# Scores and value products of two softmax branches grouped by pair of heads, in the attention of the second block

## The chip, the cores and the metric

One Trainium2 chip, one core. The time is the device time of one execution of the whole program in microseconds (us); less is better. Engines are named as in the profile: PE is the matrix engine, PEld its weight loads, DVE the vector engine, ACT the scalar engine, POOL and SP the two others. SBUF is the working memory beside the engines, PSUM the eight banks into which PE writes.

## The reference

Three layers over 256 positions of width 1024: two hybrid layers, then one block of another make. The change lies in that last block. Its mixer has two groups of eight heads of 64. The first group has three branches whose outputs are summed with gates:

```python
p_c = _masked_softmax(einsum('bsgrd,bgnd->bgrsn', qg, kc) * scale, mask_c)       # 15 compressed keys
...
p_s = _masked_softmax(einsum('btgrd,bgtkd->bgrtk', q_b, kg) * scale, mask_s)     # selected blocks
o_s = einsum('bgrtk,bgtkd->btgrd', p_s, vg)
...
p_w = _masked_softmax(einsum('btgrd,bsgd->bgrts', q_b, kwb) * scale, mask_w)     # window
o_w = einsum('bgrts,bsgd->btgrd', p_w, vwb)
...
o = gt[:, :, 0] * o_cmp + gt[:, :, 1] * o_s + gt[:, :, 2] * o_w
```

With 256 positions the four blocks of 64 are all selected and the window of 512 holds everything, so both softmax branches are causal attention over the same 256 positions, each with keys and values of its own. The second group (DSA) scores every position with an indexer, keeps the 64 best for each query, and attends to those. Both groups' outputs go through `w_out`, a norm and a residual, and then a SwiGLU feed-forward part.

## The kernel before

**Products.** Large projections are made as three products of split numbers (hi·hi, lo·hi, hi·lo; lines 276 to 278), 128 x 512 each, with weights that are loaded as `raw`, split into `hi` by ACT (L129) and into `lo` by DVE (L130). They add up in PSUM banks of the pool `acc` (four banks). Scores go to the pool `sc` (two banks, `bank()`), transposes to the pool `pt` (one bank, `bank2()`), and the outputs of a pair of heads to half a bank, `ob`.

**The heads of the first group.** The loop of L1249 takes a pair of heads `j` at a time, and first makes the product of the compressed branch (L1253) into `ob`. That product needs `cp`, which a chain of small steps makes for each half `t` of the positions: scores (L1228), maximum, exponential (L1235), gate (L1241), two transposes of `ce` (L271) into `pt`, copy (L1245). The one buffer `ce` is cleared anew for the second half (L1225). Then for each of the two softmax branches `br`: `pair_scores` makes the scores of two heads, 64 rows of PE's array each (L634 the first 128 queries, L643 the others); `softmax2` adds the mask and takes the maximum on DVE (L339) and the exponential on ACT (L340); a reciprocal and a gate follow (L1261, L1262); `scaled` multiplies, by DVE (L583) and ACT (L581) in turn; `transposed` makes three transposes into `pt` (L271) and a copy to SBUF (ACT, L617, buffer `ptsb`, three of them); `pair_values` makes the value products of the two heads, 64 columns of the array each (L590, L592). One step of the top-64 search of the indexer (DVE, L1209 and L1210) is laid in after each head. `put_pair` (L571 ACT, L572 DVE) takes the result out of `ob`.

**What sets the order.** [...] `pair_scores` and `pair_values` have a raised priority so that their products stay together. Products of other work are laid between them, "fills" below: the query projection of the second group (`dsa_queries`, 48 products into two `acc` banks, called at `j == 2` but placed earlier where it can be) and, later, the output projection (`out_proj`, L1300). After the eight pairs (the loop of L1271 does the same for the second group, with keys `kD`) come the end of `out_proj`, the norms (L928 to L959), and the feed-forward part.

Of the kernel before, what the change touches and what calls it, by code (L numbers as in the profile page):

```python
# [10 lines left out]
F32 = mybir.dt.float32  # L11
# [160 lines left out]
def body(ctx: ExitStack, tc: tile.TileContext, io, out):  # L172
    nc = tc.nc
    V, A, G, T = nc.vector, nc.scalar, nc.gpsimd, nc.tensor
# [16 lines left out]
    def tmp(n=1152):  # L191
        return ln_p.tile([128, 1152], F32, tag="y", name="y")[:, :n]
# [74 lines left out]
    mask = cst[:, C_MASK:C_MASK + 256]  # L267
# [308 lines left out]
    def scaled(e, r, ap):  # L576

        mix[0] += 1
        for t, c in ((0, slice(0, 128)), (1, slice(128, 384))):
            if mix[0] % 2 == 0:  # L580
                A.activation(e[:, c], e[:, c], AF.Copy, scale=r[:, t:t + 1])  # L581
            else:
                V.tensor_scalar(e[:, c], e[:, c], r[:, t:t + 1], None, op0=OP.mult)  # L583
        return transposed(e, ap, False)

    def pair_values(o, pts, v, c0, first, last):

        with tc.high_priority(offset=PRIO):
            for h in (1, 0):
                T.matmul(o[64 * h:64 * h + 64, :], v[:, 0, c0[h]:c0[h] + 64], pts[h][:, 0:256], start=first, stop=False)  # L590
            for h in (1, 0):
                T.matmul(o[64 * h:64 * h + 64, 128:256], v[:, 1, c0[h]:c0[h] + 64], pts[h][:, 256:384], start=False, stop=last)  # L592
# [10 lines left out]
    def pv(o, pt, vb, c0, c1):  # L603
# [2 lines left out]
        T.matmul(o[:, 1, :], pt[:, 128:256], vb[:, 0, c0:c1], start=True, stop=False)  # L606
        T.matmul(o[:, 1, :], pt[:, 256:384], vb[:, 1, c0:c1], start=False, stop=True)

    def transposed(e, ap, eng):
        b = bank2()  # L610
        for i in range(3):
            tr(b[:, i * 128:(i + 1) * 128], e[:, i * 128:(i + 1) * 128])
        pt = ap.tile([128, 384], F32, tag="ptsb", name="ptsb", bufs=3)
        if eng:
            V.tensor_copy(pt, b[:, :384])
        else:
            A.activation(pt, b[:, :384], AF.Copy)  # L617
        return pt
# [7 lines left out]

    last_read = []

    def pair_scores(q, k):

        s = [bank(), bank()]
        with tc.high_priority(offset=PRIO):
            for h in range(2):
                m = T.matmul(s[h][:, 0:128], q(h)[:, 0:128], k(h)[:, 0:128], start=True, stop=True)  # L634
                if h == 0:

                    for i in last_read:
                        tc.add_manual_dep(m.ins, i.ins.name,
                                          mybir.DependencyInfo(mybir.DependencyClass.Sync, mybir.DependencyReason.DATA),
                                          reason="pair")  # L640
                    last_read.clear()
            for h in range(2):
                T.matmul(s[h][:, 128:384], q(h)[:, 128:256], k(h)[:, 0:256], start=True, stop=True)  # L643
        return s

    def softmax2(s, bm, ap, sm):

        e = ap.tile([128, 384], F32, tag="e", name="e", bufs=4)
        nm = small(2)
        softmax_rows(e[:, 0:128], s[:, 0:128], bm[:, 128:256], nm[:, 0:1], sm[0])  # L650
        last_read.append(softmax_rows(e[:, 128:384], s[:, 128:384], bm, nm[:, 1:2], sm[1]))
        return e
# [329 lines left out]
    cos2 = cst[:, C_COS2:C_COS2 + 32].rearrange("p (t c) -> p t c", t=2)  # L982
    sin2 = cst[:, C_SIN2:C_SIN2 + 32].rearrange("p (t c) -> p t c", t=2)
    with tc.tile_pool(name="at2", bufs=1, reuse_waits="tile") as ap:
        hdT = XT()

        def rope2(dst, src, t, n):
# [25 lines left out]
        kSW = ap.tile([128, 2, 256], F32, name="kSW")  # L1013
        vSW = ap.tile([128, 2, 384], F32, name="vSW")
        kc2 = ap.tile([128, 2, 2, 256], F32, tag="kc", name="kc2")
        nq = ap.tile([128, 4, 256], F32, tag="nq", name="nq")
# [37 lines left out]
        def hidden(i, run):  # L1054

            fl = tmp(512).rearrange("p (l c) -> p l c", l=16)
            G.memset(fl[:, :, 30:32], 0.0)
            base = kc2[:, i]
            for g in range(2):
                src = bass.AP(tensor=base.tensor, offset=base.offset + 256 * g,  # L1060
                              ap=[list(base.ap[0]), [2, 16], [16, 15]])
                V.tensor_tensor(fl[:, :, 15 * g:15 * g + 15], src,
                                prm[:, P_PE + 16 * i:P_PE + 16 * i + 16, None].to_broadcast([128, 16, 15]), op=OP.add)

            pp = bank()
            for n in range(16):
                s = n % 4
                T.matmul(pp[32 * s:32 * s + 32, :128], fl[:, n, :], c1[i][:, 128 * n:128 * n + 128], start=n < 4, stop=n >= 12)
            part = ap.tile([128, 128], F32, tag="part", name="part")
            A.activation(part, pp[:, :128], AF.Copy)  # L1070
            ph = bank()
            T.matmul(ph[:, :32], part, cst[:, C_S:C_S + 32], start=True, stop=True)
            run()
            gx = ap.tile([128, 4, 30], F32, tag="gx", name="gx", bufs=2)
            x_, u_, e_, h_ = gx[:, 0], gx[:, 1], gx[:, 2], gx[:, 3]
            V.tensor_scalar(x_, ph[:, :30], prm[:, P_B1 + i:P_B1 + i + 1], None, op0=OP.add)
            V.tensor_tensor(u_, x_, x_, op=OP.mult)
            V.tensor_scalar(u_, u_, 0.044715, 1.0, op0=OP.mult, op1=OP.add)
            V.tensor_tensor(u_, u_, x_, op=OP.mult)
            A.activation(e_, u_, AF.Tanh, scale=math.sqrt(2.0 / math.pi))  # L1080
            V.tensor_scalar(e_, e_, 1.0, 0.5, op0=OP.add, op1=OP.mult)
            V.tensor_tensor(h_, e_, x_, op=OP.mult)
            return h_
# [139 lines left out]
        for t in range(2):  # L1223
# [18 lines left out]
            b = bank2()  # L1242
# [6 lines left out]
        for j in range(4):  # L1249
            if j == 2:  # L1250
                dq = dsa_queries()
            o = obank2()
            T.matmul(o, vcD[:, 2 * (j % 2):2 * (j % 2) + 2, :].rearrange("p s c -> p (s c)"), cp[:, j // 2, :],  # L1253
                     start=True, stop=False)
            for br in range(2):
                ss = pair_scores(lambda h: nq[64 * h:64 * h + 64, j, :], lambda h: kSW[64 * h:64 * h + 64, br, :])
                pts = []
                for h in range(2):
                    sm = small(4)
                    e = softmax2(ss[h], mask, ap, (sm[:, 0:1], sm[:, 1:2]))  # L1260
                    V.reciprocal(sm[:, 2:4], sm[:, 0:2])  # L1261
                    V.tensor_tensor(sm[:, 2:4], sm[:, 2:4], gw[:, :, 8 * (1 + br) + 2 * j + h], op=OP.mult)  # L1262
                    pts.append(scaled(e, sm[:, 2:4], ap))
                    next(top, None)
                pair_values(o, pts, vSW, (128 * (1 + br), 128 * (1 + br) + 64), False, br == 1)
            put_pair(hdT, j, o)

        for _ in top:
# [2 lines left out]
        for j in range(4):  # L1271
            o = obank2()
            ss = pair_scores(lambda h: dq[64 * h:64 * h + 64, j, :], lambda h: kD[64 * h:64 * h + 64, j, :])
            pts = []
# [126 lines left out]
```

## Time and profile before

| | us |
|---|---|
| median of three runs | 968.99 (968.64 to 971.33) |
| the profiled execution | 970.08 |
| its span, first to last instruction | 968.3 |
| PE busy in the span | 935.5 (97%) |
| DVE, ACT busy | 687.4 (71%), 567.8 (59%) |
| mean granted clock of PE | 0.991 of full speed |

The busy times are those of one profiled execution. The scores of the first pair begin at 697.9 us, the last product of `out_proj` is at 768.8 us, and the feed-forward part takes up the rest; what the change moves lies nearly all in these 71 us. Where PE is busy without a gap, the time goes by its work; where it waits, the trace names the instruction it waited for.

### The profile page before, as it was taken

To read this page: it belongs to the slowest core of one execution; us is meant where nothing else is said; L and a number is where in the kernel's file an instruction comes from. 1 tells how busy PE (TensorE), PEld (TensorE's weight loads), DVE (VectorE), ACT (ScalarE), POOL (GpSimd) and SP (SyncE) were. 2 spreads that over 40 slices of the span, in tenths; PEclk is the share of its full clock that TensorE was granted. 3 is DMA by queue.
4 is the path that set the end of the run, shared out by engine and by line. 5 is a ranking of instruction groups with operands and counts; after the bars stand their busy time and mean duration, and the time that the engine had idled before them with its cause. 6 is when DMAs were issued, how large, how long until landed. Compare 5 with 4: busy or idle time off the path is not lost. (4 is left out here: it accounts for less than half of the span.)

```text
span 968.3 us, 14604 instructions
## 1 busy us (share of the span) xinstructions
PE 935.5 (97%) x5418; PEld 785.1 (81%) x5418; DVE 687.4 (71%) x1487; ACT 567.8 (59%) x1143; POOL 28.8 (3%) x54
## 2 busy tenths in 40 slices
PE   8999999999999999999999999889999899999997
PEld 6888688888887888878888888788666698888886
DVE  4648788878788757668877565787788676565654
ACT  4657665555454577656455554555589745454642
POOL 0000010000000100000000000101000100000000
PEclk9999999999999999999999999999999989999999
DMA  9755548887874533447876575365312255546441
GB/s 319 288 100 217 197 175 303 292 296 271 307 253 174 193 131 130 153 176 282 301 284 217 175 255 181 109 238 207 137 45 88 66 174 184 207 169 211 154 163 44
DMA packets 33450, 190.45 MB, mean 197 GB/s; under 512 B 3696, under 2 KB 5346, under 8 KB 15842
## 3 DMA queue, kind: packets, MB, share of 16 engines
q1 hardware_dynamic: 31224, 183.75, 53.5%
q10 hardware_dynamic: 2154, 5.75, 2.1%
q8 instruction: 43, 0.70, 0.3%
q14 instruction: 29, 0.24, 0.1%
HBM read 188.17 MB, written 1.32 MB: 196 GB/s over the span
## 5 line engine op out<-in xcount | busy, mean ns | idle before, releaser
L130 DVE TENSOR_TENSOR lo<-raw,hi 128x1024 fp32r<-128x1024 f32 (+3 forms) x284 | 336.7, 1201 | 92.0 <-ACT hi L129 86.9
L129 ACT ACTIVATE hi<-raw 128x1024 fp32r<-128x1024 f32 (+3 forms) x284 | 290.2, 1038 | 104.7 <-PE acc L278 70.0
L292 PE MATMUL sc<-xh,hi 128*128 128x512 f32 x648 | 198.4, 395 | 0.0
L276 PE MATMUL acc<-hi,xh 128*128 128x512 f32 (+4 forms) x384 | 135.6, 355 | 0.7 <-ACT hi L129 0.7
L277 PE MATMUL acc<-lo,xh 128*128 128x512 f32 (+4 forms) x384 | 134.3, 350 | 0.6 <-DVE lo L130 0.6
L278 PE MATMUL acc<-hi,xh 128*128 128x512 f32 (+4 forms) x384 | 133.7, 350 | 0.7 <-DVE xh L322 0.7
L287 PEld LDWEIGHTS sc<-xh,lo 128*128 128x128 f32 x648 | 110.4, 188 | 21.2
L287 PE MATMUL sc<-xh,lo 128*128 128x256 f32 x648 | 116.0, 281 | 0.0
L292 PEld LDWEIGHTS sc<-xh,hi 128*128 128x128 f32 x648 | 104.9, 189 | 6.8
L276 PE MATMUL acc<-hi,hh 128*128 128x512 f32 x264 | 103.1, 390 | 0.0
L277 PE MATMUL acc<-lo,hh 128*128 128x512 f32 x264 | 103.0, 390 | 0.0
L278 PE MATMUL acc<-hi,hl 128*128 128x512 f32 x264 | 102.6, 390 | 0.0
L292 PE MATMUL pt<-xh,hi 128*128 128x512 f32 x312 | 97.7, 394 | 0.0
L276 PEld LDWEIGHTS acc<-hi,xh 128*128 128x128 f32 x384 | 74.8, 195 | 8.3 <-issue 1.5
L277 PEld LDWEIGHTS acc<-lo,xh 128*128 128x128 f32 x384 | 74.8, 195 | 6.8 <-DVE lo L130 1.4
L278 PEld LDWEIGHTS acc<-hi,xh 128*128 128x128 f32 x384 | 74.3, 194 | 6.5 <-DVE xh L322 1.7
L340 ACT ACTIVATE e<-e,sm 128x128 f32<-128x128 f32 (+1 forms) x128 | 56.8, 446 | 12.0 <-DVE sm L339 7.3
L287 PEld LDWEIGHTS pt<-xh,lo 128*128 128x128 f32 x312 | 53.1, 188 | 10.2
L276 PEld LDWEIGHTS acc<-hi,hh 128*128 128x128 f32 x264 | 49.5, 188 | 11.3 <-ACT hh L481 1.0
L277 PEld LDWEIGHTS acc<-lo,hh 128*128 128x128 f32 x264 | 49.6, 188 | 10.6
L278 PEld LDWEIGHTS acc<-hi,hl 128*128 128x128 f32 x264 | 49.5, 188 | 10.5 <-DVE hl L482 0.3
L414 DVE CUSTOM_DVE_ANT_0 ada<-ada,csil 128x1024 f32<-128x1024 f32 x48 | 56.2, 1220 | 0.0
(287 smaller groups left out, 1302.2 us busy)
## 6 DMA issues: line engine op xcount, KB each, us to landing
raw<-in_w_gate SPq DMA_DIRECT2D x33, 1024.0 KB, 4.9
raw<-in_w_up SPq DMA_DIRECT2D x33, 1024.0 KB, 4.9
raw<-in_w_down SPq DMA_DIRECT2D x33, 1024.0 KB, 4.8
ada<-in_w_ada SPq DMA_DIRECT2D x48, 512.0 KB, 5.7
raw<-in_w_o SPq DMA_DIRECT2D x8, 1024.0 KB, 5.1
raw<-in_w_inaqk SPq DMA_DIRECT2D x6, 1024.0 KB, 5.0
raw<-in_w_inbqk SPq DMA_DIRECT2D x4, 1024.0 KB, 6.9
gb<-in_lnrows ACTq DMA_DIRECT2D x4, 1024.0 KB, 7.1
```

The lines of the kernel that those rows point to most:

```text
L129: self.nc.scalar.activation(hi[:, :n], t[:, c], AF.Copy)
L130: self.nc.vector.tensor_tensor(lo[:, :n], t[:, c], hi[:, :n].bitcast(F32), op=OP.subtract)
L276: T.matmul(dst, lh, rh, start=start, stop=False)
L277: T.matmul(dst, lh, rl, start=False, stop=False)
L278: T.matmul(dst, ll, rh, start=False, stop=stop)
L287: T.matmul(dst[:, 0:256], ws[i][1], xT.hi[:, k0 + i, :], start=False, stop=False)
L292: T.matmul(dst, ws[i][0], xT.pair(k0 + i), start=k0 + i == 0, stop=k0 + i == 7)
L340: A.activation(e, e, AF.Exp, bias=nm, scale=-1.0, accum_out=sm)
L414: V.tensor_tensor_reduce(out=w, in0=w, in1=csil, scale=1.0, scalar=0.0, op0=OP.mult, op1=OP.add, accum_out=modc[:, g:g + 1])
```

## The change

The scores of both branches of a pair go in one run: those of branch 0 to the two `sc` banks, those of branch 1 to two banks of `acc`, held to follow by an added order (`follow`). The four softmaxes come next, and after them the value products of both branches in one run of eight, branch 1 ahead of branch 0. `ptsb` gets a fourth buffer in the second block, and to pay for it `part`, a small tile in the making of the compressed keys, takes a place in the ring `tmp` of three.

```diff
@@ -606,11 +606,13 @@
         T.matmul(o[:, 1, :], pt[:, 128:256], vb[:, 0, c0:c1], start=True, stop=False)
         T.matmul(o[:, 1, :], pt[:, 256:384], vb[:, 1, c0:c1], start=False, stop=True)
 
+    ptsb = [3]
+
     def transposed(e, ap, eng):
         b = bank2()
         for i in range(3):
             tr(b[:, i * 128:(i + 1) * 128], e[:, i * 128:(i + 1) * 128])
-        pt = ap.tile([128, 384], F32, tag="ptsb", name="ptsb", bufs=3)
+        pt = ap.tile([128, 384], F32, tag="ptsb", name="ptsb", bufs=ptsb[0])
         if eng:
             V.tensor_copy(pt, b[:, :384])
         else:
@@ -626,12 +628,18 @@
 
     last_read = []
 
-    def pair_scores(q, k):
+    last_score = [None]
+
+    def pair_scores(q, k, bank=bank, follow=False):
 
         s = [bank(), bank()]
         with tc.high_priority(offset=PRIO):
             for h in range(2):
                 m = T.matmul(s[h][:, 0:128], q(h)[:, 0:128], k(h)[:, 0:128], start=True, stop=True)
+                if h == 0 and follow:
+                    tc.add_manual_dep(m.ins, last_score[0].ins.name,
+                                      mybir.DependencyInfo(mybir.DependencyClass.NoSync, mybir.DependencyReason.DATA),
+                                      reason="pair")
                 if h == 0:
 
                     for i in last_read:
@@ -640,7 +648,7 @@
                                           reason="pair")
                     last_read.clear()
             for h in range(2):
-                T.matmul(s[h][:, 128:384], q(h)[:, 128:256], k(h)[:, 0:256], start=True, stop=True)
+                last_score[0] = T.matmul(s[h][:, 128:384], q(h)[:, 128:256], k(h)[:, 0:256], start=True, stop=True)
         return s
 
     def softmax2(s, bm, ap, sm):
@@ -982,6 +990,7 @@
     cos2 = cst[:, C_COS2:C_COS2 + 32].rearrange("p (t c) -> p t c", t=2)
     sin2 = cst[:, C_SIN2:C_SIN2 + 32].rearrange("p (t c) -> p t c", t=2)
     with tc.tile_pool(name="at2", bufs=1, reuse_waits="tile") as ap:
+        ptsb[0] = 4
         hdT = XT()
 
         def rope2(dst, src, t, n):
@@ -1066,7 +1075,7 @@
             for n in range(16):
                 s = n % 4
                 T.matmul(pp[32 * s:32 * s + 32, :128], fl[:, n, :], c1[i][:, 128 * n:128 * n + 128], start=n < 4, stop=n >= 12)
-            part = ap.tile([128, 128], F32, tag="part", name="part")
+            part = tmp(128)
             A.activation(part, pp[:, :128], AF.Copy)
             ph = bank()
             T.matmul(ph[:, :32], part, cst[:, C_S:C_S + 32], start=True, stop=True)
@@ -1252,17 +1261,20 @@
             o = obank2()
             T.matmul(o, vcD[:, 2 * (j % 2):2 * (j % 2) + 2, :].rearrange("p s c -> p (s c)"), cp[:, j // 2, :],
                      start=True, stop=False)
+            ss = [pair_scores(lambda h: nq[64 * h:64 * h + 64, j, :], lambda h: kSW[64 * h:64 * h + 64, br, :], b, br == 1)
+                  for br, b in ((0, bank), (1, acc))]
+            pts = [[], []]
             for br in range(2):
-                ss = pair_scores(lambda h: nq[64 * h:64 * h + 64, j, :], lambda h: kSW[64 * h:64 * h + 64, br, :])
-                pts = []
                 for h in range(2):
                     sm = small(4)
-                    e = softmax2(ss[h], mask, ap, (sm[:, 0:1], sm[:, 1:2]))
+                    e = softmax2(ss[br][h], mask, ap, (sm[:, 0:1], sm[:, 1:2]))
                     V.reciprocal(sm[:, 2:4], sm[:, 0:2])
                     V.tensor_tensor(sm[:, 2:4], sm[:, 2:4], gw[:, :, 8 * (1 + br) + 2 * j + h], op=OP.mult)
-                    pts.append(scaled(e, sm[:, 2:4], ap))
+                    pts[br].append(scaled(e, sm[:, 2:4], ap))
                     next(top, None)
-                pair_values(o, pts, vSW, (128 * (1 + br), 128 * (1 + br) + 64), False, br == 1)
+
+            for br in (1, 0):
+                pair_values(o, pts[br], vSW, (128 * (1 + br), 128 * (1 + br) + 64), False, br == 0)
             put_pair(hdT, j, o)
 
         for _ in top:
```

PE at the start of the heads. `sc_7034` and `sc_7035` are the scores of the first pair, `acc_7261` is the query projection of the second group, `ce` belongs to the compressed branch. Before:

```order
L1228 MATMUL sc_7012<-kcB_6352,nq_6347 128x32 x4
L276 MATMUL acc_7261<-hi_6891,xh_4674 128x512
L277 MATMUL acc_7261<-lo_6892,xh_4674 128x512
L278 MATMUL acc_7261<-hi_6891,xh_4674 128x512
L634 MATMUL sc_7034<-kSW_6344,nq_6347 128x128
L643 MATMUL sc_7034<-kSW_6344,nq_6347 128x256
L276 MATMUL acc_7261<-hi_6895,xh_4674 128x512
L277 MATMUL acc_7261<-lo_6896,xh_4674 128x512
L278 MATMUL acc_7261<-hi_6895,xh_4674 128x512
```

After, with `acc_7040` and `acc_7041` the scores of branch 1 and `e` the exponentials of the first two heads:

```order
L651 MATMUL sc_7034<-kSW_6344,nq_6347 128x256
L271 MATMUL pt_7006<-cst_88,ce_6987 128x128 x2
L638 MATMUL sc_7035<-kSW_6344,nq_6347 128x128
L651 MATMUL sc_7035<-kSW_6344,nq_6347 128x256
L638 MATMUL acc_7040<-kSW_6344,nq_6347 128x128
L638 MATMUL acc_7041<-kSW_6344,nq_6347 128x128
L651 MATMUL acc_7040<-kSW_6344,nq_6347 128x256
L651 MATMUL acc_7041<-kSW_6344,nq_6347 128x256
L271 MATMUL pt_7029<-cst_88,ce_7010 128x128 x2
L1262 MATMUL ob_87<-cp_6986,vcD_6353 128x256
L271 MATMUL pt_7057<-cst_88,e_7047 128x128 x3
L271 MATMUL pt_7078<-cst_88,e_7068 128x128 x3
```

The fills have left this place (26 of the 48 stood ahead of the first transposes of `e`); the first of them now stands behind the third transposes of `e`.

PE at the third pair. `pt` are transposes, `y` the queries of the second group, `acc_7732` to `acc_7734` fills. Before:

```order
L271 MATMUL pt_7355<-cst_88,e_7345 128x128 x3
L278 MATMUL acc_7732<-hi_7257,xh_6339 128x512
L276 MATMUL acc_7733<-hi_7257,xh_6339 128x512
L277 MATMUL acc_7733<-lo_7258,xh_6339 128x512
L634 MATMUL sc_7441<-kSW_6344,nq_6347 128x128
L634 MATMUL sc_7442<-kSW_6344,nq_6347 128x128
L643 MATMUL sc_7441<-kSW_6344,nq_6347 128x256
L643 MATMUL sc_7442<-kSW_6344,nq_6347 128x256
L271 MATMUL pt_7375<-cst_88,e_7365 128x128 x3
L278 MATMUL acc_7733<-hi_7257,xh_6339 128x512
L277 MATMUL acc_7734<-lo_7254,xh_6339 128x512
L278 MATMUL acc_7734<-hi_7253,xh_6339 128x512
```

After:

```order
L277 MATMUL acc_7733<-lo_7258,xh_6339 128x512
L278 MATMUL acc_7733<-hi_7257,xh_6339 128x512
L271 MATMUL pt_7361<-cst_88,e_7351 128x128 x3
L271 MATMUL pt_7381<-cst_88,e_7371 128x128 x3
L271 MATMUL pt_7401<-cst_88,e_7391 128x128 x3
L271 MATMUL pt_7421<-cst_88,e_7411 128x128 x3
L276 MATMUL acc_7734<-hi_7253,xh_6339 128x512
L590 MATMUL ob_87<-ptsb_7425,vSW_6345 64x256
L590 MATMUL ob_87<-ptsb_7405,vSW_6345 64x256
```

The transposes of the four heads, which had fills and scores between them, stand in a row.

ACT at the same place, where each `ptsb` copy sets the one `pt` bank free. Before:

```order
L340 ACTIVATE e_7395,sm_7394<-e_7395,sm_7396 128x256
L617 ACTIVATE ptsb_7359<-pt_7355 128x384
L340 ACTIVATE e_7415,sm_7414<-e_7415,sm_7416 128x128
L340 ACTIVATE e_7415,sm_7414<-e_7415,sm_7416 128x256
L617 ACTIVATE ptsb_7379<-pt_7375 128x384
L581 ACTIVATE e_7415<-e_7415,sm_7414 128x128
L581 ACTIVATE e_7415<-e_7415,sm_7414 128x256
```

After:

```order
L1010 ACTIVATE dq_7240<-pt_7331 128x4x128
L619 ACTIVATE ptsb_7365<-pt_7361 128x384
L340 ACTIVATE e_7454,sm_7453<-e_7454,sm_7455 128x128
L340 ACTIVATE e_7454,sm_7453<-e_7454,sm_7455 128x256
L619 ACTIVATE ptsb_7385<-pt_7381 128x384
L340 ACTIVATE e_7474,sm_7473<-e_7474,sm_7475 128x128
L340 ACTIVATE e_7474,sm_7473<-e_7474,sm_7475 128x256
L619 ACTIVATE ptsb_7405<-pt_7401 128x384
L581 ACTIVATE e_7474<-e_7474,sm_7473 128x128
L619 ACTIVATE ptsb_7425<-pt_7421 128x384
L581 ACTIVATE e_7474<-e_7474,sm_7473 128x256
```

The copies of the four heads now have the exponentials and the scaling of the next pair between them.

## Rows read from the trace of the kernel before

**Rows 1.** Busy us (instructions) by stage: PE, PEld, DVE, ACT, POOL; clock; DMA.

```profile
694.80:706.90 12.10, 12.10 (x68) 8.96 (x68) 8.43 (x47) 4.79 (x16) 0.00 (x0) 1.00 0.01 2
706.90:745.30 38.40, 37.55 (x245) 24.22 (x243) 34.70 (x174) 35.57 (x112) 0.00 (x0) 1.00 0.23 83
745.30:769.20 23.90, 23.42 (x136) 16.43 (x135) 14.08 (x46) 18.81 (x54) 0.86 (x2) 1.00 0.21 67
```

**Rows 2.** Waits of PE from 694 to 770 us: total, times, longest.

```profile
PE ob L590 <- ACT ptsb L617: 0.8, 2, 0.6
PE pt L271 <- ACT ptsb L617: 0.5, 2, 0.3
```

**Rows 3.** Timeline, PE, start of the heads: start, us, what, [idle before].

```profile
695.91 0.48 PE L278 MATMUL acc<-hi,xh 128*128 128x512 f32 x1
...
700.24 0.40 PE L276 MATMUL acc<-hi,xh 128*128 128x512 f32 x1
700.47 0.38 PE L271 MATMUL pt<-cst,ce 128*128 128x128 f32 x2
...
705.17 0.40 PE L276 MATMUL acc<-hi,xh 128*128 128x512 f32 x1
705.50 0.49 PE L634 MATMUL sc<-kSW,nq 64*128 64x128 f32 x4
705.83 0.60 PE L643 MATMUL sc<-kSW,nq 64*128 64x256 f32 x4
706.36 0.70 PE L1253 MATMUL ob<-cp,vcD 128*128 128x256 f32 x2
706.89 0.49 PE L271 MATMUL pt<-cst,e 128*128 128x128 f32 x3
707.14 0.48 PE L277 MATMUL acc<-lo,xh 128*128 128x512 f32 x1
707.46 0.39 PE L278 MATMUL acc<-hi,xh 128*128 128x512 f32 x1
```

**Rows 4.** Timeline, DVE: the chain of the compressed branch.

```profile
698.60 0.28 DVE L1241 TENSOR_TENSOR ce<-ce,sm 128x120 f32<-128x120 f32 x1
...
700.95 0.17 DVE L1225 MEMSET ce<- 128x136 f32 x1 [2.07 <-PE pt L271]
```

**Rows 5.** Timeline, PE: transposes that waited for the copy of the pt bank.

```profile
708.32 0.55 PE L271 MATMUL pt<-cst,e 128*128 128x128 f32 x3 [0.23 <-ACT ptsb L617]
...
752.63 0.55 PE L271 MATMUL pt<-cst,e 128*128 128x128 f32 x3 [0.31 <-ACT ptsb L617]
```

**Rows 6.** Timeline, ACT: scaling, copies of pt to ptsb, exponentials.

```profile
706.70 0.80 ACT L581 ACTIVATE e<-e,sm 128x128 f32<-128x128 f32 x2 [0.61 <-DVE sm L1262]
...
752.11 0.47 ACT L617 ACTIVATE ptsb<-pt 128x384 f32<-128x384 f32 x1
752.48 0.39 ACT L340 ACTIVATE e<-e,sm 128x128 f32<-128x128 f32 x1
...
752.86 0.50 ACT L340 ACTIVATE e<-e,sm 128x256 f32<-128x256 f32 x1
...
753.35 0.47 ACT L617 ACTIVATE ptsb<-pt 128x384 f32<-128x384 f32 x1
```

**Rows 7.** Timeline, ACT, at the end of the output projection.

```profile
763.79 1.06 ACT L129 ACTIVATE hi<-raw 128x1024 fp32r<-128x1024 f32 x1 [0.50 <-PE acc L278]
```

**Rows 8.** Timeline, DVE, at the end of the output projection.

```profile
764.89 1.23 DVE L130 TENSOR_TENSOR lo<-raw,hi 128x1024 fp32r<-128x1024 f32 x1 [1.14 <-ACT hi L129]
```

**Rows 9.** Timeline, PE: first product of the feed-forward part.

```profile
771.87 1.32 PE L271 MATMUL sc<-cst,y 128*128 128x128 f32 x8 [2.66 <-DVE y L941]
```

**Rows 10.** Busy us by stage, columns as in Rows 1, around that gap.

```profile
768.80:772.00 3.20, 0.54 (x3) 0.13 (x2) 2.61 (x5) 3.20 (x8) 1.72 (x3) 1.00 0.00 0
773.00:780.00 7.00, 6.59 (x30) 6.10 (x29) 6.16 (x10) 2.15 (x6) 1.08 (x2) 0.52 0.00 0
780.00:783.00 3.00, 3.00 (x27) 3.00 (x27) 1.71 (x4) 2.04 (x3) 0.00 (x0) 0.99 0.52 156
```

## The prediction

> **What bounds the kernel now.** I read first the busy times by stage, from the first scores to the end of the output projection [rows 1]. PE is busy for 12.10 of 12.10 us, then 37.55 of 38.40, then 23.42 of 23.90: it is the bound, and nothing that another engine does faster can help unless it makes PE's own work shorter. PE gets this density from the fills between the short products of the heads. Then the waits [rows 2]: PE waited in this stretch for one kind of instruction, the ACT copy of the transposes to `ptsb`, 0.8 us ahead of value products and 0.5 us ahead of transposes. No wait for scores, softmax banks or a transfer stands in the table. So the change, which takes entries out of PE's order and moves the rest, can gain only what PE spends on going from one kind of product to another, and can lose whatever cover the heads have today.
>
> **The joins.** The order shows eleven pieces of score runs in the four pairs before and six after, eight value runs before and four after, and one cut run of the second group made whole: ten joins. Their price is read at one run [rows 3]: a fill is followed by the next product 0.23 us later (700.24 to 700.47), but by a score run 0.33 later (705.17 to 705.50), and the first fill after another kind takes 0.32 (707.14 to 707.46) where a fill takes 0.23. So an entry costs 0.10 and an exit about 0.1: 0.2 us at the least. Inside the run the 128-wide part takes 0.33 and the 256-wide part 0.53; the difference, 0.20, is 128 columns, so that 0.13 and 0.13 of them are fixed. A join that saves the entry and both fixed parts saves 0.36. I take 0.29, between the two, for scores and values alike: 10 x 0.29 = 2.9, with ends 2.0 and 3.6.
>
> **The front.** Here the order changes most. Before, 26 fills stood between 695.91 and 705.17 [rows 3], 26 x 0.23 = 6.0 us of PE's work under the chain of the compressed branch and the first softmaxes. After, branch 1 of the first two pairs takes the `acc` banks, and the first fill stands behind the third transposes of `e`. The fills aren't lost, they run later, but the time that they covered must be found elsewhere. Some comes back, since the chain no longer queues behind them: the gated `ce` was done at 698.88 [rows 4] and its transposes ran at 700.47 [rows 3], 1.6 us later; the clearing of the buffer for the second half waited 2.07 us for that [rows 4]; and at the later links I find a further 1.3. I walk the first transposes of `e` 2.9 us earlier than 706.89. The net loss there is 6.0 - 2.9 = 3.1 us, its own join counted, so nine joins, 2.6, stay for the sum.
>
> **Second to fourth heads.** The second transposes of `e` came 1.43 us after the first [rows 3, 5] with three fills between. Their input is scaled by ACT from 706.70, two pieces of 0.7 and 0.8 [rows 6], so ready about 1.3 us after the first transposes began; with no fill there, that stands open: 1.3. The fourth transposes need the one `pt` bank, and the copy that frees it is queued on ACT behind seven instructions, of 0.37 to 0.8 each [rows 6], some 3.0 us together, with four fills (0.9) between: 2.1. The value products of the first pair and three other places wait for a copy or a bank at once; the nearest row is the 0.8 in two such waits [rows 2], 0.35 to 0.4 each: 1.4 for four.
>
> **The third pair.** Its twelve transposes stand in a row. Each set of three needs the bank that the copy ahead frees, and on ACT two exponentials stand between two copies: 0.37 + 0.38 + 0.49 = 1.24 from copy to copy (752.11 to 753.35) [rows 6], while a set of transposes takes 0.3. Two such steps leave 0.95 each, the third, behind half a scaling, 0.8, the first 0.2; and the values behind the last copy wait 0.52 as other users of the bank did after a copy began (752.11 to 752.63) [rows 5, 6]: 3.4. The fourth pair has two waits of that kind, 0.7 and 0.4: 1.1. Who waits for ACT there is PE alone, and behind PE all fills of the output projection.
>
> **What goes.** The waits of the stretch before, 38.40 - 37.55 = 0.85 [rows 1], are replaced: -0.8. Some 15 fills that were the first after another kind of product now follow a fill: 15 x 0.09 [rows 3] = 1.4. And at the end of the output projection a weight split on ACT [rows 7] and its other half on DVE, 1.23 us [rows 8], stand ahead of the first half's norm; after, they stand behind it. Of the wait of 2.66 for that norm [rows 9] I take 0.7 off, since the second half's chain still needs the last products; ends 0 and 1.2.
>
> **The clock.** [...] The gaps that I walk at the front are about 1 us each, between short products; no row shows such a stretch at less than 1.00. The sum has nothing for it.
> [...]
>
> **Edits at nothing.** The fourth `ptsb` buffer: the four copies of a pair fit, and no wait for a `ptsb` buffer is in the table [rows 2]. `part` in the ring of three may wait for its turn; nearest are the two `ptsb` waits on PE, 0.5 together [rows 2], so 0 to 0.5 either way, 0 taken, since other steps lie between its users. SP and POOL keep their order; weight loads that a later split sets free start later, and DMA engines are busy 0.01 to 0.23 of these stages [rows 1], so there is room to catch up; if not, PE would wait at the first product of the late weight.
>
> **The sum.** 3.1 + 1.3 + 2.1 + 1.4 + 3.4 + 1.1 = 12.4; less 0.8, 2.6, 1.4 and 0.7 = 5.5: +6.9 us. Against the profiled execution, 970.08 us for a span of 968.3, that is 977.0; the profiled run lies 1.1 above the median of the three, 968.99, and against the median it is **975.9 us**.
>
> **The rivals.** Differences within 0.3% (2.9 us, 966.1 to 971.9) cannot be told from no change here.
>
> A: the sum as it stands, 975.9, with 973.5 to 978.5 from the ends of its terms. For it: PE is strictly in order, and the places are in the order. Against it: the waits of the third pair hang on ACT being just then where I walk it.
>
> B: the joins pay and the cover is found. If the branch 1 scores are read out of `acc` early, ACT and DVE, which have slack at the front (4.79 and 8.43 busy of 12.10 [rows 1]), may run the whole chain so much earlier that the 6.0 us are regained. Place: the front; price: the loss of 3.1 and the later waits vanish, -2.6 - 0.3 - 0.7 = -3.6, so 965.4, faster. It decides if the first transposes of `e` come 6 us earlier rather than 2.9. Against: the chain is a row of small DVE and ACT steps whose own lengths no join shortens.
>
> C: the front alone. ACT and DVE, with less of PE's work between their inputs, get ahead by the third pair, and the copies are done when PE asks. Then 3.1 + 1.3 - 2.6 - 0.7, and half of the fill term, -0.7, give +0.4: 969.4, no change. For it: ACT is busy 35.57 of 38.40 in the middle stage [rows 1], but half of its work there would be shifted; against it: the copies are queued behind exponentials of the next pair in ACT's order, however early ACT comes.
>
> D: A with a slow stretch of the clock in the thin front. In the slow stretch 30 products took 6.59 us, in the one behind it 27 took 3.00 [rows 10]: 0.22 and 0.11 each, so 3 us for a stretch of that kind: 978.9. For it: the gap row [rows 9, 10]; against it: PE is never silent for 2.66 us at the front.
> [...]
>
> **How the numbers follow.** A 0.45, D 0.20, C 0.22, B 0.13. The time is A's. The range leaves out B and the upper tail of D, and takes in C: 967.5 to 981.0; A's own with D is 973.5 to 981.0. Faster by over 0.3%: B and little else, 0.14; within: C, 0.21; slower: A and D, 0.65.
>
> **What the profile after would show.** Right: PE's waits in the first pairs' transposes on ACT L581 and `ptsb`, some 3 us at the third pair, busy share of PE in the front stage near a half, clock 1.00. Joins: value runs of eight with no gap. Rival D: granted clock about 0.5 after the front. Rival C: gaps at the front only. Rival B: PE busy throughout, first transposes of `e` near 701. The prediction is wrong if the waits on the one `pt` bank don't appear, or if a fill stands where I see none.

## The result, and the profile after

The changed kernel takes 979.86 us in the median of five runs (977.05 to 980.42), the kernel before 969.89 (five runs). The ratio is 1.0086, with a 95% interval from 1.0068 to 1.0105: slower by 0.86%, some 8.3 us (the two medians lie 10.0 apart). Forecast were 975.9 us, +6.9, with a range from 967.5 to 981.0. The profiled run of after is the one of 977.05 us, span 975.3.

The two traces are compared from the first product of the compressed branch's scores (695.10 us before, 694.45 after) to the first product of the feed-forward part (771.87 and 779.06), here called the head stage. Busy times by stage, columns as in Rows 1, of before:

```profile
695.10:771.87 76.77, 72.78 (x444) 49.33 (x443) 59.00 (x267) 61.72 (x186) 2.46 (x5) 1.00 0.18 63
```

and of after, the whole stage and four pieces of it (the front up to the first transposes of `e`, from there to the first fills at full speed, the third pair's transposes, and the rest):

```profile
694.45:779.06 84.61, 76.70 (x443) 53.34 (x441) 58.23 (x265) 60.80 (x183) 1.94 (x4) 0.90 0.16 57
694.45:704.59 10.14, 7.90 (x40) 5.69 (x39) 7.90 (x45) 4.18 (x14) 0.00 (x0) 0.65 0.00 1
704.59:711.27 6.68, 5.81 (x28) 3.99 (x26) 4.79 (x34) 5.24 (x20) 0.00 (x0) 0.50 0.02 4
736.44:742.50 6.06, 3.45 (x19) 1.99 (x21) 5.30 (x31) 4.87 (x17) 0.00 (x0) 0.95 0.38 157
742.50:779.06 36.56, 35.07 (x212) 24.21 (x208) 22.66 (x78) 28.61 (x83) 1.94 (x4) 0.96 0.20 73
```

The stage is 7.84 us longer (84.61 for 76.77). PE stood idle 7.91 us in place of 3.99, and was busy 76.70 in place of 72.78, with the same products but at a mean granted clock of 0.90 in place of 1.00. So half of the loss shows as gaps and half as products that take longer. In the records of these two traces the granted clock is 1.00 or 0.50 (in after 0.50 from 697.55 to 711.21 us and 1.00 from there to 741.92), so a mean between them is a stretch that has both. The waits of PE from 690 to 785 us in after, of which 0.7 and 1.4 us are no news (the indexer's scores, and the feed-forward part that had 2.66 [rows 9]):

```profile
PE pt L271 <- ACT ptsb L619: 2.2, 3, 0.9
PE sc L271 <- DVE y L949: 1.4, 1, 1.4
PE pt L271 <- DVE ce L1250: 1.2, 1, 1.2
PE acc L278 <- DVE xh L322: 1.0, 1, 1.0
PE pt L271 <- ACT e L581: 0.9, 1, 0.9
PE sc L638 <- ACT rl L1203: 0.7, 3, 0.3
PE sc L638 <- DVE ce L1239: 0.6, 1, 0.6
...
PE acc L276 <- DVE r L1002: 0.5, 1, 0.5
```

Where [rows 2] had one releaser, the copy to `ptsb`, PE now waits for the chain of the compressed branch (L1250, L1239), for the scaling of the second head (L581), and 2.2 us instead of 0.5 for copies ahead of transposes. The timeline of PE at the front (transposes, first fill), which answers to [rows 3, 5]:

```profile
698.38 0.66 PE L271 MATMUL pt<-cst,ce 128*128 128x128 f32 x2 [1.21 <-DVE ce L1250]
...
704.59 0.85 PE L271 MATMUL pt<-cst,e 128*128 128x128 f32 x3
706.31 1.08 PE L271 MATMUL pt<-cst,e 128*128 128x128 f32 x3 [0.87 <-ACT e L581]
707.33 0.80 PE L638 MATMUL sc<-kSW,nq 64*128 64x128 f32 x4
...
708.77 0.64 PE L638 MATMUL acc<-kSW,nq 64*128 64x128 f32 x4
...
710.19 0.90 PE L271 MATMUL pt<-cst,e 128*128 128x128 f32 x3
710.74 0.69 PE L276 MATMUL acc<-hi,xh 128*128 128x512 f32 x1
...
711.96 0.49 PE L271 MATMUL pt<-cst,e 128*128 128x128 f32 x3
```

The first transposes of `e` come 10.14 us after the start of the stage (11.79 before), the fourth set (711.96) 17.51 us after it; before, the fourth set stood at 712.62, 17.52 us after it. At the same distance PE had then done 34 fills before and 4 after. Thirty fills at 0.23 are 6.9 us. The other work differs by two runs: after has made the scores of both branches of the second pair (707.33, 708.77), before those of branch 0 alone, which is one score run (0.75, by the like run at 726.99 to 727.74 in after); and before has made one value run that after has not (0.80). The front has lost 6.9 - 0.75 + 0.8 = 7.0 us.

The clock of the front, by stretches of 2 us of after:

```profile
695.00:697.00 2.00, 2.00 (x16) 1.72 (x15) 1.53 (x7) 0.61 (x2) 0.00 (x0) 1.00 0.01 4
697.00:699.00 2.00, 0.79 (x3) 0.29 (x2) 1.09 (x5) 0.00 (x0) 0.00 (x0) 0.64 0.00 0
699.00:701.00 2.00, 1.45 (x9) 1.35 (x9) 1.39 (x7) 0.69 (x2) 0.00 (x0) 0.50 0.00 0
709.00:711.00 2.00, 2.00 (x12) 1.35 (x11) 1.99 (x16) 1.66 (x7) 0.00 (x0) 0.50 0.04 8
711.00:713.00 2.00, 2.00 (x12) 1.60 (x11) 2.00 (x16) 2.00 (x10) 0.00 (x0) 0.95 0.02 4
```

It falls in the first gap and is back where the fills begin, a slow stretch of 13.7 us (697.55 to 711.21). The timeline of PE at the third pair's twelve transposes in after:

```profile
736.44 0.55 PE L271 MATMUL pt<-cst,e 128*128 128x128 f32 x3 [0.22 <-ACT dq L1010]
737.57 0.55 PE L271 MATMUL pt<-cst,e 128*128 128x128 f32 x3 [0.58 <-ACT ptsb L619]
738.82 0.55 PE L271 MATMUL pt<-cst,e 128*128 128x128 f32 x3 [0.70 <-ACT ptsb L619]
740.31 0.55 PE L271 MATMUL pt<-cst,e 128*128 128x128 f32 x3 [0.95 <-ACT ptsb L619]
741.24 0.50 PE L276 MATMUL acc<-hi,xh 128*128 128x512 f32 x1 [0.38 <-DVE sm L339]
```

### The profile page after: what moved, and what is told of

It is laid out like the page before. It is cut to its first block, busy times and chain, and to the rows that moved or that the text cites. A ratio compares the mean times of both kernels' runs of the same rounds, so it can differ in the third digit from the quotient of the medians.

```text
span 975.3 us, 14604 instructions
## 1 busy us (share of the span) xinstructions
PE 936.9 (96%) x5418; PEld 785.2 (81%) x5418; DVE 687.6 (71%) x1487; ACT 568.4 (58%) x1143; POOL 28.1 (3%) x54
## 5 line engine op out<-in xcount | busy, mean ns | idle before, releaser
L292 PE MATMUL sc<-xh,hi 128*128 128x512 f32 x648 | 198.4, 395 | 0.0
L276 PE MATMUL acc<-hi,xh 128*128 128x512 f32 (+4 forms) x384 | 133.5, 349 | 2.2 <-ACT hi L129 1.2
L278 PE MATMUL acc<-hi,xh 128*128 128x512 f32 (+4 forms) x384 | 132.0, 345 | 1.3 <-DVE xh L322 1.3
L292 PEld LDWEIGHTS sc<-xh,hi 128*128 128x128 f32 x648 | 104.9, 189 | 6.8
L292 PE MATMUL pt<-xh,hi 128*128 128x512 f32 x312 | 97.7, 394 | 0.0
L276 PEld LDWEIGHTS acc<-hi,xh 128*128 128x128 f32 x384 | 73.3, 191 | 10.3 <-ACT hi L129 2.1
L278 PEld LDWEIGHTS acc<-hi,xh 128*128 128x128 f32 x384 | 73.0, 190 | 7.3 <-DVE xh L322 2.4
```

Of the source, the lines that this page charges most:

```text
L276: T.matmul(dst, lh, rh, start=start, stop=False)
L278: T.matmul(dst, ll, rh, start=False, stop=stop)
L292: T.matmul(dst, ws[i][0], xT.pair(k0 + i), start=k0 + i == 0, stop=k0 + i == 7)
```

## The experiments

Twelve kernels were run, one of them the changed kernel once more, each beside the kernel before on the same chip. The chip is not the same for all twelve, so kernels are compared by their ratios. "Ratio" is to the kernel before, with its 95% interval. "Stage" is the head stage of the profiled run, one trace for each kernel: 76.77 us before and 84.61 after. The edits are shown against after unless said otherwise, and cut where "..." stands.

**`part` alone.** To the kernel before:

```diff
-            part = ap.tile([128, 128], F32, tag="part", name="part")
+            part = tmp(128)
```

> The kernel before with one edit of the change alone: the small tile `part` takes a place in the ring of three. In the trace after, PE stood 0.65 us ahead of the trace before at the start of the heads (694.17 against 694.82 us for the same transposes), and nothing else of the change lies ahead of that point. Theory F (the loss is at the front and in the third pair, `part` is a small gain): 0.4 to 0.7 us under the kernel before. Rival (the lead comes from later priorities, not from `part`): no difference, below 0.2 us, and the wait for `part` still stands in the table of waits.

Measured: 970.86 us, ratio 0.999 (0.9979 to 1.0002). No difference, and the stage of its trace begins at 695.57 us, not earlier than in before. The lead of 0.65 us in the trace of after was not `part`'s; a second trace of after, below, begins the stage at 695.99, so it was a difference from trace to trace. PE's wait of 0.4 for `part` was gone, so the rival was wrong on that point, but no time came of it.

**Joined values alone.** The scores of each branch apart, in the two `sc` banks; the value products of a pair stay in one run at its end:

```diff
-            ss = [pair_scores(..., b, br == 1) for br, b in ((0, bank), (1, acc))]
             pts = [[], []]
             for br in range(2):
+                ss = pair_scores(lambda h: nq[64 * h:64 * h + 64, j, :], lambda h: kSW[64 * h:64 * h + 64, br, :])
                 for h in range(2):
```

> The changed kernel with its scores as before (each branch apart, in the two sc banks); the value products stay joined, branch 1 ahead of branch 0, with four ptsb buffers and `part` in the ring. The fills are back at the front in the order. Theory F (front cover and clock are the loss): 965.5 to 968.5 us, that is the kernel before less 0.65 for `part` and about 1 for four joins; granted clock 1.00 at the front. Rival T (the joined values put copies and exponentials in the wrong order on ACT, and that is most of the loss): 972 or more, with waits of PE on the ptsb copies of 3 us and more.

Measured: 972.53 us, ratio 1.0019 (1.0003 to 1.0035), stage 77.67 us at a granted clock of 1.00. That is 4 us above theory F's range, which fails, and just inside the time that the rival named (972 or more). But the rival's waits of 3 us and more are not there, and a ratio of 1.0019 is a small part of after's 1.0086, so the joined values are not most of the loss. PE's busy time in the stage fell from 72.78 to 72.04, 0.74 for four joins or 0.19 each; the waits took more than that back: for copies to `ptsb`, value products waited 1.5 us (two waits) and transposes 1.1 (four), where [rows 2] has 0.8 and 0.5.

**Joined in the third and fourth pair alone.** The next three kernels differ from this one in the condition alone.

```diff
+            if j < 2:
+                for br in range(2):
+                    ss = pair_scores(...)
...
+                    pair_values(o, pts, vSW, (128 * (1 + br), 128 * (1 + br) + 64), False, br == 1)
+            else:
+                ss = [pair_scores(...) for br, b in ((0, bank), (1, acc))]
...
```

> The changed kernel with the first two pairs as before, joined in the third and fourth pair alone. The fills are back at the front in the order. Theory F: the front's share goes and the third pair's stays: 968 to 973 us, granted clock 1.00 at the front, waits on ptsb copies near 2 us. Rival (the front is not the main share): 975 or more.

Measured: 969.58 us, ratio 0.9987 (0.9976 to 0.9998), stage 75.55 us, clock 1.00. Without the two first pairs the loss is gone, and a little is won: the joins pay 1.45 us of busy time, the gap ahead of the feed-forward part is 1.39 instead of 2.66, and new waits take back part of it. The expected waits of near 2 us on `ptsb` copies were 0.7: in this order no row of twelve transposes stands at the third pair, so the kernel does not test that place. It is the fastest of the kernels here, by a margin that its interval barely parts from none.

**Joined in the first two pairs alone.**

```diff
-            if j < 2:
+            if j >= 2:
```

> The changed kernel with joins in the first two pairs alone; the third and fourth pair as before. Theory F: the front loses as in the changed kernel, gaps of about 3 us and a slow stretch of the clock of some 12 us; the third pair's row of waits goes. 973 to 978 us. Rival T (the third pair is most of the loss): within 2 us of the kernel before.

Measured: 976.93 us, ratio 1.0053 (1.0037 to 1.0068), stage 82.65 us with a mean clock of 0.92. The front alone costs 5.9 us of stage. Together with the late pairs' -1.2 that would make +4.7, not +7.84: the row of twelve transposes and the slow stretch behind it exist only where both are joined.

**Joined in the first pair alone.**

```diff
-            if j < 2:
+            if not (j == 0):
```

In the order seven fills then stand between its scores and its transposes.

> The changed kernel with the first pair alone joined, the other three as before. In the order seven fills stand between its scores and the first transposes of `e`, where the changed kernel has none and the kernel before 26 ahead of them. Theory F (missing fills make the front thin): a part of the loss of the kernel with two joined pairs (5.1 us): 972 to 975, with a slow stretch at the front shorter than there. Rival (the four softmaxes in a row, not the fills, hold PE up): as with two joined pairs, 976 or more.

Measured: 974.15 us, ratio 1.0032 (1.0020 to 1.0044), stage 79.71 us, clock 0.96. No pair joined, one, two: 76.77, 79.71, 82.65 us of stage, about 2.9 for each. The time is in theory F's range and under the rival's 976. A fixed cost for each joined pair, whatever its cause, would give the same half; for the fills speaks that the wait of 0.87 for the second head's scaling [L581] is gone in this trace, where fills now stand ahead of those transposes. And the slow stretch of the clock is shorter (0.50 from 701 to 707 us).

**Joined in the fourth pair alone.**

```diff
-            if j < 2:
+            if not (j == 3):
```

> The changed kernel with the fourth pair alone joined, the first three as before. All fills stand where the kernel before has them up to the third pair. Theory F: one score join and one value join, 0.3 + 0.2, and the shorter gap ahead of the feed-forward part, 1.3, are won and nothing lost: 968.5 to 970.5, 0.1 to 0.3% under the kernel before. Rival (the gain of the kernel with two late pairs was the run of luck of its clock, with no slow stretch at the feed-forward part): no difference from the kernel before, within 0.5 us.

Measured: 971.02 us, ratio 1.0010 (0.9996 to 1.0023): no difference, as the rival had it. One score join and one value join can't be told from nothing here, although its gap ahead of the feed-forward part, too, was 1.4 us and its clock 1.00.

**Joined scores, values apart.**

```diff
-            for br in (1, 0):
-                pair_values(o, pts[br], vSW, ..., False, br == 0)
+                pair_values(o, pts[br], vSW, ..., False, br == 1)
```

> The changed kernel with joined scores, but the value products of each branch apart, as before. Theory F: the scores alone take the acc banks and push the fills away, so the loss stays: 975 to 981 us, with the slow stretch at the front. Rival T (the joined values are the cause): within 3 us of the kernel before.

Measured: 979.04 us, ratio 1.0077 (1.0051 to 1.0104), stage 84.53 us. The joined scores, with the banks they take, carry the loss; no kernel here parts the joining from the banks.

**The query projection first.** `dq = dsa_queries()` ahead of the loop, all joins kept:

```diff
         top = topk()
+        dq = dsa_queries()

         for j in range(4):
-            if j == 2:
-                dq = dsa_queries()
```

> The changed kernel with the query projection of the second group called ahead of the loop over the pairs, so that it takes its two acc banks first; all joins stay. The first pair's branch 1 takes the other two banks, the second pair's must wait until the projection has been read. In the order the first fill is back at the place it had before. Theory F: front gaps and the slow stretch of the clock go, 969 to 974 us. Rival R (the slow clock or the gaps come from the joined runs themselves, not from the missing fills): the granted clock is about 0.5 there again and the time 976 or more. A wait of the second pair's scores for the banks, 1 to 4 us, would be a cost of this kernel's own.

Measured: 980.64 us, ratio 1.0087 (1.0071 to 1.0103), stage 89.10 us. Theory F in its simple form fails here. The time lies in the range of rival R (976 or more), and the clock was low at the front, as R had it. The fills stood at the front, in the order as in before, and PE was busy there throughout. But then they were used up. Its timeline of PE from the last fill on:

```profile
715.99 0.39 PE L278 MATMUL acc<-hi,xh 128*128 128x512 f32 x1
...
719.86 0.63 PE L271 MATMUL pt<-cst,y 128*128 128x128 f32 x4 [2.61 <-DVE y L1003]
721.18 0.58 PE L271 MATMUL pt<-cst,e 128*128 128x128 f32 x3 [0.69 <-ACT dq L1010]
722.34 0.90 PE L271 MATMUL pt<-cst,e 128*128 128x128 f32 x3 [0.58 <-ACT ptsb L619]
723.83 0.90 PE L271 MATMUL pt<-cst,e 128*128 128x128 f32 x3 [0.58 <-ACT ptsb L619]
725.31 0.90 PE L271 MATMUL pt<-cst,e 128*128 128x128 f32 x3 [0.58 <-ACT ptsb L619]
726.79 1.12 PE L590 MATMUL ob<-ptsb,vSW 128*64 128x256 f32 x4 [0.58 <-ACT ptsb L619]
```

No fill stands between the transposes of a pair in the first two pairs; each set but a pair's first waits for the copy of the one before (six waits, 4.0 us), and the projection's own chain on DVE shows (2.61). Behind that gap the clock was at 0.50 again, from 722 to 732 us (means of 0.66, 0.50 and 0.82 in the three stretches of 5 us from 720). The kernel before spreads its 48 fills over both pairs. The clock was also low from 694 to 704 us (0.56 from 694 to 696, 0.50 from 696 to 700, 0.55 from 700 to 705), before anything that the edit changes on PE: at the first transposes of `ce`, with the same products ahead of them, this trace was 9.62 us into the stage and before 5.37 [rows 3]. These 4.25 us of its 12.3 may not be the edit's. Without them it would still lie above theory F's range of 969 to 974.

**Extra products at the front.**

```diff
             b = bank2()
+            for _ in range((5, 2)[t]):
+                T.matmul(b, hT.hi[:, 0, 0:128], hT.pair(0), start=True, stop=True)
             for j in range(2):
                 tr(b[:, j * 128:j * 128 + 128], ...)
```

> The changed kernel with seven extra products of 128x512 that nothing uses, five ahead of the first and two ahead of the second transposes of the compressed branch, into the pt bank that these transposes then overwrite. They add work to PE only where it waits. It parts the clock from the missing cover: if the slow stretch is the price of the thin front, the granted clock there stays at 1.00 or is slow for a shorter time, and the kernel is 1.5 to 4 us faster than the changed one; if the clock costs nothing because PE waits for the other engines there anyway, the time stays within 1 us of the changed kernel, or rises by the 1.6 us of the products.

Measured: 977.56 us, ratio 1.0058 (1.0036 to 1.0081); the changed kernel once more, on the same chip:

> The changed kernel once more, on the same chip as the others, as their yardstick: 977 to 980.5 us as in its five runs, with two places where the granted clock can be low, the front of the heads and the start of the feed-forward part. If the runs of 979 to 980 have a slow stretch at the feed-forward part that the profiled run of 977.05 had not, their mean clock is about 0.003 lower, as the runs listed so far have it.

980.13 us, ratio 1.0083 (1.0052 to 1.0114), stage 84.82 us, its clock low at the front (0.50 from 700 to 710 us) and behind the third pair (0.51 from 743 to 746), as in the first trace of after; the start of the feed-forward part ran at 1.00. The expected explanation of its spread, a slow stretch there, thus found no support. The two traces part earlier: 1.54 of the 1.7 us between their spans lie ahead of the stage. There the granted clock was 0.97 from 600 to 650 us in the first and 0.90 in the second, with the same products and two gaps of like length (3.1 and 2.3 us in the first, 3.2 and 2.2 in the second). With seven products more the median is 2.6 us lower, though the two intervals overlap with four runs each, and the stage is 83.56 us. Busy times by 2 us of the kernel with extra products:

```profile
705.00:707.00 2.00, 1.03 (x5) 0.69 (x5) 2.00 (x15) 1.38 (x5) 0.00 (x0) 1.00 0.00 0
707.00:709.00 2.00, 1.71 (x9) 1.19 (x11) 1.24 (x10) 2.00 (x8) 0.00 (x0) 0.67 0.00 0
709.00:711.00 2.00, 2.00 (x14) 1.26 (x10) 1.85 (x13) 1.46 (x7) 0.00 (x0) 0.50 0.03 8
711.00:713.00 2.00, 1.82 (x11) 1.21 (x10) 2.00 (x16) 2.00 (x8) 0.00 (x0) 0.98 0.02 4
```

The clock stays at 1.00 until about 11 us into the stage (3 in after), falls behind the 2 us in which PE was busy for half, and the fourth transposes come 16.01 us after the start of the stage (17.51 in after). That is 1.5 us for a slow stretch of 3.4 us in place of 13.7; the other 5.5 of the 7.0 stay.

**The third pair's copies on DVE.** In after, and in the kernel with extra products:

```diff
-                    pts[br].append(scaled(e, sm[:, 2:4], ap))
+                    pts[br].append(scaled(e, sm[:, 2:4], ap, j == 2))
...
-        return transposed(e, ap, False)
+        return transposed(e, ap, dve)
```

> The changed kernel with the ptsb copies of the third pair on DVE instead of ACT; the order on PE keeps its twelve transposes in a row. In the changed kernel PE waited there 0.58, 0.70 and 0.95 us on the ptsb copies, and 3 us later the granted clock fell to 0.5 for some 5 us. Theory F2 (the copies stand behind the next pair's exponentials on ACT, and the idle row brings the second slow stretch): these waits shrink below 0.4 each, and 2 to 4 us are won against the changed kernel: 976 to 978. Rival (the one pt bank itself sets the pace, whoever copies; or DVE is late there): waits of the same size on DVE, within 1 us of the changed kernel.

Measured: 979.05 us, ratio 1.0078 (1.0056 to 1.0100), the stage 84.99 us: no gain on after. Its timeline of PE there:

```profile
738.25 0.55 PE L271 MATMUL pt<-cst,e 128*128 128x128 f32 x3 [0.22 <-ACT dq L1010]
739.45 0.55 PE L271 MATMUL pt<-cst,e 128*128 128x128 f32 x3 [0.65 <-DVE ptsb L617]
740.65 0.55 PE L271 MATMUL pt<-cst,e 128*128 128x128 f32 x3 [0.65 <-DVE ptsb L617]
741.85 0.55 PE L271 MATMUL pt<-cst,e 128*128 128x128 f32 x3 [0.65 <-DVE ptsb L617]
```

The sets follow at 1.20 us, where after has 1.13, 1.25 and 1.49. On DVE no exponential of the next pair stands between the copies, and still the one `pt` bank lets a set through in 1.20 us: transposes, copy, transposes. The queue on ACT was a small part of the wait; that the sets stand in a row without a fill was the large one. The slow stretch of the clock behind it was there as before (means of 0.85 from 740 to 745 us and 0.81 from 745 to 750). Theory F2 falls, its rival holds.

> The changed kernel with both remedies, the seven extra products at the front and the DVE copies of the third pair. Theory F2 (two thin places, each with gaps and a slow stretch of the clock, make the loss): the gains add, 2.5 and 2 to 4 us, to 973 to 976, and the granted clock falls below 1.00 for less than 5 us in all between the first scores and the feed-forward part. If 975 or more stays with the clock at 1.00, then gaps alone, not the clock, are the loss.

Measured: 979.50 us, ratio 1.0093 (1.0074 to 1.0112), stage 84.30 us at a mean clock of 0.96. The gains did not add, as the copies on DVE had brought none. In this trace the clock was 1.00 at the whole front, and yet:

```profile
712.94 0.40 PE L276 MATMUL acc<-hi,xh 128*128 128x512 f32 x1
714.86 0.55 PE L271 MATMUL pt<-cst,e 128*128 128x128 f32 x3 [1.52 <-ACT ptsb L619]
```

The fourth transposes, at 15.78 us of the stage, waited 1.52 us for the copy, at a clock of 1.00; in after, behind 13.7 us at 0.50, they had no wait (711.96). That ACT catches up behind a slow PE is a reading of these two traces, which no run shows by itself; by it the clock costs less at the front than the length of its slow stretch says. Behind the third pair it was at 0.50 for 6.8 us (means of 0.81 from 740 to 745 us and 0.51 from 745 to 750), where the kernel with extra products alone has 3.4. Against that kernel the stage is 0.7 us longer, and the median 1.9 higher; but they ran on different chips, and the intervals of their ratios overlap (1.0036 to 1.0081, 1.0072 to 1.0112), so that a difference is not shown.

## Why the prediction was right, and where not

**The way and the size.** Slower, +6.9 forecast, +8.3 measured by the ratio (10.0 between the medians; the two traces, of runs of 970.08 and 977.05 us, differ by 7.84 in the stage); the case that it was built on, missing cover at the front and at the third pair, is what the runs showed: joined scores alone carry the loss (1.0077), the late pairs alone have none (0.9987), and it grows by 2.9 us of stage with each early pair.

**The front.** The terms for it (3.1, 1.3, 2.1 and about 0.5 of the 1.4) made 7.0, and 7.0 were lost. That the sums agree is partly luck, for the parts were less well placed. The first transposes of `e` came 1.65 us earlier rather than 2.9; 2.66 earlier in the kernel with extra products, where the clock was still full. The second set waited 0.87 where 1.3 was reckoned. The fourth set did not wait in after, where 2.1 was reckoned, and waited 1.52 in the last experiment told above, at full clock. The traces suggest that in after the low clock took the place of that wait; no run shows it by itself.

**The clock.** The sum had nothing for it, as "no row shows such a stretch at less than 1.00", and the profile was to show 1.00; rival D had 3 us at a chance of 0.20. This step failed: D's slow stretch came on top of A's gaps, at 0.50 for 13.7 us at the front, and in every trace with joined first pairs but the last told above. PE's busy share there was 0.78 (7.90 of 10.14), not near a half, with products that took longer. The price at the front is 1.5 us by the experiment for most of the stretch, and a second slow stretch, not foreseen, follows the third pair (0.50 from 741.92 to 745.34 us): its eight value products took 2.56 us (741.68 to 744.24) where the second pair's took 1.46 (721.78 to 723.24), 1.1 more. The trace of after has 0.64 in the 2 us of the first gap, 1.21 us long, and 1.00 again from 711.21 us, once the fills run (the first starts at 710.74). By itself it does not settle when the clock falls: see the last section. The reason against D, that PE is never silent for 2.66 us, did not hold.

**The third pair.** 3.4 reckoned, 0.22 + 0.58 + 0.70 + 0.95 + 0.38 = 2.8 measured. The place was right, the reason half wrong: with the copies on DVE, free of ACT's exponentials, the one bank still sets a pace of 1.2 us. The 1.1 for the fourth pair did not come.

**The joins.** 0.29 each was reckoned. Values: 0.74 of busy time for four, 0.19 each. Two late pairs: 1.45 for two value joins and their score runs, so that scores are worth more, about 0.5 for each pair. In sum near the 2.9. The 1.4 taken off for some 15 fills that now follow a fill was too much: the runs of fills in the stage fall from 33 to 24, and nine at 0.09 are 0.8, most of it in the front.

**The end of the output projection.** The gap fell from 2.66 to 1.38, 1.3 us where 0.7 was taken. Little was won behind it: from the first product of the feed-forward part to its first product of L292 the trace has 17.48 us before and 17.26 after, although the clock was 0.50 for 6.9 us there in before [rows 10] and 1.00 in after. PE was busy 1.8 us less (15.28 for 17.05), but the order of the first transposes had changed, and two waits took 1.5 of it back (before has one there, of 0.40):

```profile
782.06 0.39 PE L278 MATMUL acc<-hi,xh 128*128 128x256 f32 x1 [0.96 <-DVE xh L322]
...
787.47 1.29 PE L271 MATMUL sc<-cst,y 128*128 128x128 f32 x8 [0.96 <-DVE y L949]
```

**Still open.** From the start of the stage to that product of L292 after is 7.6 us longer. The front (7.0), the third pair (2.8), its slow stretch (1.1) and the wait for L1002 (0.5), less nine joins at the forecast's price (2.6), the old waits outside the front (0.6), two runs of fills fewer there (0.2) and the end (1.5), make 6.5. About 1 us is not put to an instruction. Of the spread of the runs of after, 977.05 to 980.42, the two traces show the part that lies ahead of the stage; why the clock differed there is open.

## What to carry to other kernels

Fills are a stock: a kernel whose PE is full by means of them has a fixed number, here 48 of the query projection. Joining the short products of a chain, with the PSUM banks that it took from the fills, moved them here to where they covered nothing: 34 were done ahead of the fourth transposes before, 4 after. Before joining, count what stands between the dependent steps, and join only where another stock is at hand: here the two late pairs, beside the output projection, could be joined without loss, the two early ones cost 2.9 us of stage each. Check who owns the bank when transposes come to stand in a row, before blaming the engine that empties it: here a set took 1.20 us with the copies on DVE, 1.13 to 1.49 with them on ACT.

## What the runs showed of the hardware that was not expected

The granted clock fell at gaps much shorter than the 2.66 us ahead of the feed-forward part: in after in a gap of 1.21 us behind short score products (0.50 from 697.55 us on). In the kernel with the query projection first it fell at about 694 us behind three gaps of 0.20 to 0.30, the same ones at which the kernel before stayed at 1.00:

```profile
692.00:694.00 2.00, 1.80 (x13) 1.07 (x11) 1.86 (x6) 1.18 (x3) 0.00 (x0) 1.00 0.08 33
694.00:696.00 2.00, 2.00 (x13) 1.90 (x11) 1.51 (x6) 0.72 (x2) 0.00 (x0) 0.56 0.01 4
```

What decided between the two, no run here shows.

What a slow stretch cost here differed with what PE did in it. In the kernel with the query projection first PE had no gap at the front: 9.2 us at 0.50 put the first transposes of `ce` 4.25 us behind, nearly half of the stretch. At the thin front of after, where PE waits for other engines, a stretch shorter by some 10 us gave back 1.5 us. At the feed-forward part two kernels, that with the first pair alone joined and that with the first two, have the order of before with a slow stretch of 3.4 us rather than 6.9: there the piece of 17.48 us took 16.24 and 16.22.
